# Who orders the side engines' queues: a two-layer hybrid decoder trunk with the order planned by a timeline model

## The chip, the cores and the metric

The kernel runs on one core of a Trainium2 chip. A time is the device time of one execution in microseconds (us). The kernel before took 2891.07 us (median of two runs, 2890.86 and 2891.28). The core has one tensor engine (TensorE, "PE" in the profile), a vector engine (VectorE, "DVE"), an activation engine (ScalarE, "ACT"), GpSimd ("POOL"), and a queue engine that issues DMAs (SyncE, "SP"). Each engine runs its own list of instructions strictly in order; where it needs a result of another engine, the instruction at its head waits on a semaphore, and all behind it wait too.

## The reference, cut to what matters

```python
D_MODEL = 1024; SEQ = 1024; DEPTH = 2; CHUNK = 64     # 4 mLSTM heads and 4 retention heads of 256
def reference(x, c, positions, w_ada, b_ada, norm_g, w_in, conv_w, conv_b, ...):
    c_act = silu(c)
    for l in range(DEPTH):
        shift, scale, gate = split(c_act @ w_ada[l] + b_ada[l], 3)
        h = rmsnorm(x, norm_g[l]) * (1 + scale) + shift
        mq, mk, mv, mo, mz, mi, mf, rq, rk, rv, rz = split_cols(h @ w_in[l])
        mq, mk = split(silu(causal_dwconv(concat(mq, mk), conv_w[l], conv_b[l])), 2)
        cell = mlstm_chunkwise(mq, mk, mv, mi + b_igate[l], mf + b_fgate[l])
        y_m = sigmoid(mo) * head_layernorm(cell, gn_m[l]) * silu(mz)
        ret = retention_chunkwise(rotary(rq, positions), rotary(rk, positions), rv)
        y_r = head_layernorm(ret, gn_r[l]) * silu(rz)
        x = x + gate * (concat(y_m, y_r) @ w_out[l])
    return rmsnorm(x, final_g)
```

Everything is float32. In each chunk the two attentions compute scores q k^T, weight them, multiply by v, add the part that comes from a running state, and update that state with k^T v.

## The kernel before, in words

**Arithmetic.** A float32 product is made of three matmuls in a reduced format (fp32r): each operand is cut into a high half, a cast made by ACT (L742, `split_to`), and a low half, the operand minus its cast, made by POOL unless told otherwise (L743). Then L150, L151 and L152 (`mm3`) multiply high by high, low by high and high by low. So every operand of PE passes over ACT and then over POOL or DVE. Tiles called wH and wL are the halves of weights, cH and cL those of the attention's state, sH and sL those of its weighted scores; the tiles q and kc hold both halves of q and k.

**Projections.** The large product h @ W_in is done two column groups at a time, by a scheme with seven products in place of eight (as in Strassen's method). It needs sums and differences of the blocks of h, the forms F of a layer, built once by DVE (`build_forms`, L566 to L583, tiles b and acc), and sums of the blocks of the weights (`weight_forms`, L597 to L603), by POOL for q and k and by DVE for v and the gates. A `Feeder` keeps four of a group's weight forms ahead. Weights come by the loads L611 (`pair_forms`, tile raw) and L623 (`vpair_forms`, tile b). After each product ACT copies and DVE adds into the accumulators (L646 and L649, `combine`, traced with high priority).

**Jobs.** In each layer PE runs the first gate columns (`first`), the small products for mi and mf (`gate_units`; their weights wgr are loaded in the startup and split there, L424 and L742/L743), and then a list of jobs: v for four pairs of heads; then for heads 4 to 7 (retention) and 0 to 3 (mLSTM) the q and k projections, with one gate job between two heads. A finished q or k passes the rotary (L826 to L832) or the convolution with SiLU (L749 to L759), and is written to DRAM (L797, buffers qdr and kfr; k also in a second form, kdr). When k of a head is done, its attention is launched: a generator whose parts are woven between the PE units of the jobs that follow, by counting ticks.

**A score step.** Each head has four chunks of 256 positions. For chunk j, `fetch_qk` (L857) loads q and k back from DRAM into tiles called acc, ACT casts them (L742), and POOL takes the low halves (L743). q has two buffers, kc has one. `diagonal` (L896) and `mm3` then make the scores on PE. `fetch_kv` loads and splits v and the rows of k. DVE weights the scores (L909 to L920), PE makes the values and the state update, DVE normalises (L1007 to L1029) and `finish` multiplies in the gates and stores (L1034, L1038).

**Ahead of the jobs.** In layer 0 a startup region, an order written out by hand as a script of steps, runs the adaLN product, the first norm and the first gate columns. Then come `build_forms`, the gate chain (`gate_chain`, L454 to L529: the stabiliser of the mLSTM, with a store and a reload through DRAM at L491 and L505), in layer 0 the rotary tables (L391 to L419, from a load of the positions at L391), and the loads of the rotary tables (L840). The end of a layer is the product with W_out (`out_units`), in layer 1 also with the final norm and stores.

**What sets the order.** PE's order is written by hand for the whole kernel, and all engines' order in the startup and in the last part of layer 1:

```python
    manual = ctx.enter_context(tc.manual_schedule(engines={mybir.EngineType.PE}))   # L1256
    startup = tc.manual_schedule()                                                  # L1258
        ending = tc.manual_schedule() if l and alone else None                      # L1123, in out_units
```

Elsewhere the framework's scheduler decides in what order DVE, ACT, POOL and SP get the instructions that the program traces. It lists them by the times at which it reckons that each can start, from the dependences, the buffers that pools hand out and the priorities (which follow the order of tracing, except under `tc.high_priority()` in `combine`). The list is fixed before the run.

## Time and profile before

| | before |
|---|---|
| median of the runs | 2891.07 us |
| the profiled execution, its own time | 2891.24 us |
| its span in the profile | 2889.5 us |
| mean granted PE clock | 0.893 |
| busy PE / DVE / POOL / ACT | 2302.5 / 1826.2 / 1367.5 / 1163.1 us |
| instructions in the span | 35104 |
| DMA | 360.20 MB, mean 125 GB/s |

The profile shows one execution. "Busy" is the sum of an engine's instruction times; a PE that is held at a lower clock is busy for longer with the same work. A row of a view by instruction has the start and the duration in us, the engine, the line of the program, the operation, the output and input tiles and their shapes, and in square brackets how long the engine stood idle before it and what ended that wait ("<-ACT kc L742": the cast of kc at L742 on ACT). By stages: the startup lasts until about 142 us; layer 0 has v until 380, the retention heads until 800, the mLSTM heads until 1310 and the output product until 1445 us; the norm and the first gate columns of layer 1 last until 1582, its v until 1800, the retention heads until 2230, the mLSTM heads until 2680, and the last product, the final norm and the stores until the end.

### The profile page before, as it was taken

How to read it: one execution, taken by the hardware profiler on the slowest of the kernel's cores; microseconds unless marked ns; L12 is line 12 of the kernel's file. 1: busy time of each engine (PE TensorE's matmuls, PEld its weight loads, DVE VectorE, ACT ScalarE, POOL GpSimd, SP SyncE). 2: the span in 40 equal slices, each digit the busy share in tenths (PEclk: the TensorE clock that was granted, in tenths of full speed). 3: DMA queues.
4: the chain of work that ended last, by engine and by line, in shares of the span. 5: the costliest groups of instructions: out<-in, count | busy, mean ns of one | idle time of the engine just before them, and what ended most of it. 6: DMA issues, size and time to landing. Idle time of an engine off the chain costs nothing. (4 is left out here: it accounts for less than half of the span.)

```text
span 2889.5 us, 35104 instructions
## 1 busy us (share of the span) xinstructions
PE 2302.5 (80%) x11483; PEld 1943.4 (67%) x11483; DVE 1826.2 (63%) x3199; ACT 1163.1 (40%) x2149; POOL 1367.5 (47%) x1098
## 2 busy tenths in 40 slices
PE   4789977777676777789996999788777676767998
PEld 3589966556565556668785998666666555656777
DVE  4994356557566777877527534567567677777744
ACT  4523333333344444454345333333334444444433
POOL 0444664544545545452266446655554545544123
PEclk9899989789788888889998999899888788888999
DMA  7034344433443334347641433444343433424766
GB/s 221 25 85 123 95 118 130 117 120 107 122 123 110 114 105 129 94 132 256 220 142 33 107 99 113 121 120 118 98 127 91 111 109 110 129 82 128 234 195 173
DMA packets 483012, 360.20 MB, mean 125 GB/s; under 512 B 186866, under 2 KB 403706, under 8 KB 482828
## 3 DMA queue, kind: packets, MB, share of 16 engines
q1 hardware_dynamic: 482684, 357.70, 42.5%
q8 instruction: 90, 1.47, 0.2%
q14 instruction: 94, 0.77, 0.1%
q10 hardware_dynamic: 144, 0.26, 0.0%
HBM read 251.90 MB, written 105.94 MB: 124 GB/s over the span
## 5 line engine op out<-in xcount | busy, mean ns | idle before, releaser
L743 POOL TENSOR_TENSOR wL<-raw,wH 128x512 fp32r<-128x512 f32 x492 | 674.4, 1378 | 710.8 <-ACT wH L742 655.9
L150 PE MATMUL pp<-b,wH 128*128 128x512 f32 x1616 | 673.7, 417 | 41.6 <-ACT acc L646 36.7
L151 PE MATMUL pp<-b,wH 128*128 128x512 f32 x1616 | 664.1, 411 | 4.2 <-DVE b L1095 4.2
L152 PE MATMUL pp<-b,wL 128*128 128x512 f32 x1616 | 659.8, 408 | 0.0
L742 ACT CAST wH<-raw 128x512 fp32r<-128x512 f32 x556 | 340.4, 618 | 633.3 <-PE pp L151 269.8
L150 PEld LDWEIGHTS pp<-b,wH 128*128 128x128 f32 x1616 | 331.1, 205 | 116.3 <-ACT acc L646 43.9
L151 PEld LDWEIGHTS pp<-b,wH 128*128 128x128 f32 x1616 | 328.6, 203 | 68.9 <-DVE b L1095 5.8
L152 PEld LDWEIGHTS pp<-b,wL 128*128 128x128 f32 x1616 | 324.1, 201 | 73.8
L896 PE MATMUL pa<-q,kc 128*128 128x256 f32 x384 | 105.5, 423 | 169.5 <-POOL q L743 126.2
L150 PE MATMUL pp<-wH,b 128*128 128x256 f32 (+1 forms) x576 | 182.7, 317 | 57.4 <-ACT wH L742 44.4
L649 DVE TENSOR_TENSOR acc<-pp,acc 128x512 f32<-128x512 f32 x180 | 122.4, 681 | 149.6 <-PE pp L152 137.3
L896 PEld LDWEIGHTS pa<-q,kc 128*128 128x128 f32 x384 | 85.0, 306 | 191.3 <-POOL q L743 139.6
L151 PE MATMUL pp<-wL,b 128*128 128x256 f32 (+1 forms) x576 | 182.0, 316 | 13.2 <-POOL wL L743 13.2
L152 PE MATMUL pp<-wH,b 128*128 128x256 f32 (+1 forms) x576 | 181.4, 315 | 0.2
L150 PE MATMUL pa<-wH,b 128*128 128x256 f32 (+1 forms) x576 | 177.1, 307 | 0.0
L151 PE MATMUL pa<-wL,b 128*128 128x256 f32 (+1 forms) x576 | 176.8, 307 | 0.0
L152 PE MATMUL pa<-wH,b 128*128 128x256 f32 (+1 forms) x576 | 176.6, 307 | 0.0
L150 PEld LDWEIGHTS pp<-wH,b 128*128 128x128 f32 x576 | 113.9, 198 | 65.6 <-ACT wH L742 45.4
L754 DVE SCALAR_TENSOR_TENSOR acc<-acc,cols,acc 128x511 f32<-128x511 f32 x144 | 140.3, 974 | 27.2 <-ACT acc L749 26.1
L743 POOL TENSOR_TENSOR wL<-b,wH 128x512 fp32r<-128x512 f32 x56 | 77.3, 1381 | 159.3 <-ACT wH L742 120.4
L646 ACT COPY acc<-pp 128x512 f32<-128x512 f32 x180 | 104.2, 579 | 111.8 <-PE pp L152 106.7
L151 PEld LDWEIGHTS pp<-wL,b 128*128 128x128 f32 x576 | 114.0, 198 | 20.4 <-POOL wL L743 15.2
(348 smaller groups left out, 4954.2 us busy)
## 6 DMA issues: line engine op xcount, KB each, us to landing
raw<-in_w_in_dram SPq DMA_DIRECT2D x250, 256.0 KB
raw<-in_w_out_dram SPq DMA_DIRECT2D x128, 256.0 KB
gdr<-acc SPq DMA_DIRECT2D x64, 256.0 KB
vdr<-acc SPq DMA_DIRECT2D x64, 256.0 KB
qdr<-acc SPq DMA_DIRECT2D x64, 256.0 KB
kfr<-acc SPq DMA_DIRECT2D x64, 256.0 KB
acc<-qdr SPq DMA_DIRECT2D x64, 256.0 KB
acc<-kfr SPq DMA_DIRECT2D x64, 256.0 KB
```

The source lines that it names most:

```text
L150: PE.matmul(o, lt[0], rt[0], start=start, stop=False, skip_group_check=more)
L151: PE.matmul(o, lt[0], rt[1], start=False, stop=False, skip_group_check=more)
L152: PE.matmul(o, lt[1], rt[0], start=False, stop=stop, skip_group_check=more)
L646: A.copy(keep[n], bank["Z" if n == 3 else "X"])
L649: V.tensor_tensor(keep[m], bank[b], keep[m], ALU.add)
L742: A.copy(dst[0], src)
L743: eng.tensor_tensor(dst[1], src, f(dst[0]), ALU.subtract)
L754: V.scalar_tensor_tensor(acc[:, d:], pt[:, 0:HALF - d], wcol, acc[:, d:], ALU.mult, ALU.add)
L896: PE.matmul(pd, piece(kx[j], i, dt, tt * P, P), qd, start=dt == 0 and i == 0, stop=dt == 1 and i == 1)
```

## The change

```diff
-    with tile.TileContext(nc) as tc:
+    with tile.TileContext(nc, schedule_with_timeline_sim=True) as tc:
         tile_hybrid_trunk(tc, *args)
```

This is the whole diff (L1518). It changes what the scheduler reckons with. By default it uses a simple estimate of each instruction's length and readiness; now it plans with a model of the engines' timelines. The program that is traced is the same: the same instructions with the same operands and shapes, the same pools and buffer counts. PE's hand-written order, the startup's script and the last part of layer 1 stay as they are. What may differ is the order of the instructions on DVE, ACT, POOL and SP in all other regions, with it the order in which DMAs are issued, and which of a pool's buffers a tile gets.

## The prediction

> **What bounds the kernel now.** I read the page first, for the whole: the profiled execution took 2891.24 us, 1.7 us outside its span, and the median of the runs shown is 2891.07 us, so a sum made on this execution holds for the median.
>
> ```profile
> span 2889.5 us, 35104 instructions
> PE 2302.5 (80%) x11483; PEld 1943.4 (67%) x11483; DVE 1826.2 (63%) x3199; ACT 1163.1 (40%) x2149; POOL 1367.5 (47%) x1098
> ```
>
> No engine is full. TensorE (PE) is the busiest and its order is the one thing that does not change, so I ask next what it waits for. This is the view of waits for PE alone (total us, times, longest):
>
> ```profile
> PE pa L896 <- POOL q L743: 126.2, 32, 7.7
> PE pa L150 <- ACT kc L742: 123.1, 22, 10.3
> PE pa L976 <- ACT cH L742: 59.0, 13, 8.0
> PE pp L150 <- ACT wH L742: 44.4, 5, 22.8
> PE pa L896 <- POOL kc L743: 43.3, 32, 3.0
> PE pp L150 <- ACT acc L646: 38.7, 17, 8.8
> PE pa L152 <- POOL kc L743: 33.3, 26, 3.0
> PE pa L151 <- POOL q L743: 17.6, 18, 3.1
> ```
>
> Five of these rows are one cause: the first matmuls of a score step wait for the two halves of q and kc, which ACT casts (L742) and POOL subtracts (L743). Together 126.2 + 123.1 + 43.3 + 33.3 + 17.6 = 343.5 us in 64 score steps (8 heads, 4 chunks, 2 layers), 5.4 us each. The windows show where (us of PE, its weight loads, DVE, ACT and POOL busy, then the granted PE clock):
>
> ```profile
> 141.60:235.00 93.40, 74.09 (x551) 71.95 (x552) 81.31 (x140) 24.15 (x44) 39.48 (x26) 0.88 0.34 93
> 380.00:800.00 420.00, 309.56 (x1377) 255.82 (x1377) 246.08 (x414) 139.26 (x265) 218.96 (x173) 0.84 0.41 118
> 800.00:1310.00 510.00, 378.94 (x1721) 313.53 (x1720) 375.14 (x754) 230.12 (x450) 246.70 (x213) 0.86 0.41 118
> 1582.00:1615.00 33.00, 27.46 (x202) 26.36 (x203) 28.35 (x31) 11.61 (x22) 15.10 (x11) 0.91 0.34 78
> 1800.00:2230.00 430.00, 338.39 (x1552) 281.36 (x1551) 271.83 (x471) 163.16 (x308) 239.21 (x194) 0.88 0.40 113
> 2230.00:2680.00 450.00, 325.22 (x1439) 266.23 (x1438) 327.48 (x634) 200.39 (x397) 225.35 (x194) 0.84 0.40 114
> ```
>
> 380 to 800 and 1800 to 2230 are the retention heads, 800 to 1310 and 2230 to 2680 the mLSTM heads. There PE idles a quarter of the time and its clock is at 0.84 to 0.88, while DVE, the next busiest, stands at 59 to 74%.
>
> **Why a score step waits: queues, not work.** The stretch around one stall, PE, ACT and POOL, each in order of time:
>
> ```profile
> 497.24 0.39 PE L152 MATMUL pp<-b,wL 128*128 128x512 f32 x1
> 505.16 0.58 PE L150 MATMUL pa<-q,kc 128*128 128x256 f32 x1 [7.54 <-ACT kc L742]
> ...
> 497.66 0.60 ACT L534 ACTIVATE th<-pp 128x512 f32<-128x512 f32 x1 [1.30 <-PE pp L152]
> 498.15 1.13 ACT L742 CAST wH<-raw 128x512 fp32r<-128x512 f32 x2
> 504.49 0.61 ACT L742 CAST kc<-acc 128x512 fp32r<-128x512 f32 x1
> ...
> 498.89 2.48 POOL L743 TENSOR_TENSOR wL<-raw,wH 128x512 fp32r<-128x512 f32 x2 [11.33 <-ACT wH L742]
> 501.34 1.25 POOL L597 TENSOR_TENSOR raw<-raw,raw 128x512 f32<-128x512 f32 x1
> 502.68 1.26 POOL L598 TENSOR_TENSOR raw<-raw,raw 128x512 f32<-128x512 f32 x1
> ```
>
> POOL stood idle for 11.33 us and then ran four weight operations that are needed only later; the cast of kc waited for them, since a weight cast that needs L598 stands before it on ACT. POOL was idle because ACT's queue held an evacuation (L534) that had to wait for PE's last matmul before the score step, with two casts of weights, long ready, behind it. PE waited for ACT, ACT had waited for PE.
>
> **The change, part by part.** The work and PE's order stay; DVE, ACT, POOL and SP are put in another order. I counted in the two built programs. ACT around this stall (minus before, plus after):
>
> ```
> +L742 TensorCopy wH_4625<-raw_4617 128x512
> ...
> -L534 Activation th_4736<-pp_4511 128x512
> -L742 TensorCopy wH_4625<-raw_4617 128x512
> ...
>  L742 TensorCopy wH_4698<-raw_4617 128x512
> +L534 Activation th_4671<-acc_4642 128x512
>  L742 TensorCopy kc_4651<-acc_4649 128x512
> ```
>
> *Score steps.* For each step I followed the semaphores of the built program back from its first q or kc wait, through every queue, to the latest matmul that must have run, and counted the matmuls between that one and the waiting one. Before, 36 of the 64 steps have 0 or 1 between, so the whole off-PE chain is exposed; the median is 0. After, 8 have, and the median is 24; 45 steps gain, one loses. A stall then shrinks by the time of the added matmuls. Their step is in these rows, after a stall and once warm:
>
> ```profile
> 545.16 0.58 PE L896 MATMUL pa<-q,kc 128*128 128x256 f32 x1 [6.35 <-POOL q L743]
> ...
> 548.04 0.63 PE L150 MATMUL pp<-b,wH 128*128 128x512 f32 x1
> 548.47 0.63 PE L151 MATMUL pp<-b,wH 128*128 128x512 f32 x1
> ...
> 550.95 0.39 PE L152 MATMUL pp<-b,wL 128*128 128x512 f32 x1
> 551.17 0.39 PE L150 MATMUL pp<-b,wH 128*128 128x512 f32 x1
> ```
>
> 0.43 us start to start when cold, 0.22 when warm. I take the warm one, which gives least: 24 x 0.227 = 5.4 us against stalls of 5.4 us on average. Taken off stall by stall, never below zero, it leaves about 140 of the 343.5 us; the same count leaves 49 of the 59 us on cH and about 10 less on L646. Sum: 225 us.
>
> *The clock.* After the 6.35 us stall PE ran cold until 550.5, some 5 us at half pace, so 2.4 us more were lost. 28 steps fewer with an open chain (36 less 8), 2.4 us each: 67 us.
>
> [...]
>
> So 292 us lie open. Not all will come: if PE runs earlier, DVE must give the same work in less time. With all of it the four stretches shrink from 1810 to 1518 us and DVE's 1220 us become 80%, in mLSTM stretches over 85%. DVE can run so full (95% in the row below), but it then answers later. The bounds are 0 and 292; I take 0.7, nearer to the upper end, since DVE has room: -204 us.
>
> *Both fronts.* Here the change costs. Ahead of the first value projection of a layer, DVE builds the forms of h (L566 to L583), and the new order puts the gate chain (L468 to L490) and, in layer 0, rotary tables (L393 to L416) among them; on SP the weight loads of L623 (tile b) now stand behind the gate chain's stores and its reload (L491, L505). By the built programs 62 more DVE instructions precede the last form in layer 0, and 21 in layer 1. Their price, from two windows of DVE alone in which these kinds run:
>
> ```profile
> 138.90:192.40 53.50, 50.95 (x70) 0.88 0.30 75
> 1578.10:1608.50 30.40, 29.99 (x30) 0.84 0.27 80
> ...
> 1578.53 1.96 SPq L623 DMA_DIRECT2D b<-in_w_in_dram  x4
> ...
> 1581.56 0.62 ACT L742 CAST wH<-b 128x512 fp32r<-128x512 f32 x1 [5.61 <-DMA b<-in_w_in_dram]
> ```
>
> 0.73 us each: 62 x 0.73 = 45 us. 1.0 us each: 21 us. One more DMA on the way, 3.0 us from issue to use, each time: +3. But DVE is then done with work that today stalls PE just after: the windows from 141.6 and from 1582 hold 93.4 - 74.1 = 19.3 and 33.0 - 27.5 = 5.5 us of PE idle. Layer 0: 45 + 3 - 19 = +29. Layer 1: 21 + 3 - 5 = +19. Bounds: +72 if nothing is recovered, 0 if hidden behind PE's gate matmuls.
>
> *Startup.* The small gate weights (wgr) arrive late, and their cast and split stand early in the queues:
>
> ```profile
> 46.77 0.31 DVE L743 TENSOR_TENSOR cL<-wgr,cH 128x32 fp32r<-128x32 f32 x2 [29.61 <-ACT cH L742]
> ...
> 60.92 0.48 DVE L331 TENSOR_SCALAR b<-b,rs 128x512 f32<-128x512 f32 x1
> ...
> 48.71 0.50 SPq L391 DMA_DIRECT2D kc<-in_positions_dram  x1
> ```
>
> DVE waits 29.61 us with ready work behind. After, these stand some 30 places later, but the copy of the positions (L393) now comes right after this L331, and its load is issued only at 48.71, usable 3.0 us later, at 51.7. DVE passes that point at 61.4 today: -10 us (bounds 0 and -29.6).
>
> Sum: -204 + 29 + 19 - 10 = -166; 2891 - 166 = 2725 us.
>
> **The rivals.**
> *DVE takes the place of the queues* (0.17). The score steps get their operands, but DVE at 74% in the mLSTM stretches cannot follow, and waits on cf, sd or evacuations replace those on q. Half of my share: -102 + 38 = 2827 us. For it: DVE's rows in the windows. Against: 95% when it has ready work.
> *More comes* (0.15): all 292 us, 2891 - 292 + 38 = 2637 us. For it: I counted the added matmuls at the warm step, and later stalls shrink with earlier ones.
> *Slower* (0.12): the casts of q and kc stand so early on ACT and POOL that the reloads have not landed, and the queues stand for them, with wH, cH and sH behind. It decides from the point where a load lands after its cast's turn by more than the 5.4 us of added cover. Then the 343.5 us stay, the fronts add 38, and at half of 64 steps' 3.0 us landing another 96 come: 2929 to 3025, middle 2975 us. Against: the loads stand hardly later on SP than before.
> *Nothing reaches PE* (0.06): the order differs, but other waits end at the same time: 2891 us. Against: 945 of 3197 DVE instructions move by more than 5 places.
>
> A rule speaks for the DVE rival. The Trainium skill ("SBUF — State Buffer", Who interferes with whom) has a DVE instruction with two SBUF inputs and a GpSimd one that reads SBUF shut each other out for the whole instruction, so tighter packing would lengthen DVE. The trace bears it out:
>
> ```profile
> L566 DVE TENSOR_TENSOR acc<-b,b x32: 671/684/1780, 103.8 to 1570.0; 128x512 f32<-128x512 f32 x32
> ```
>
> The longest is 1.1 us over the median of 0.68 us, about the length of the POOL operations above (1.25 and 1.26 us).
>
> **How the numbers follow.** My forecast has 0.50, with its own range of 2650 to 2800 us. Faster or slower by about 2%, 58 us, is what a measurement of this kernel can tell: under 2833 is faster. Faster: 0.50 + 0.15 + 0.10 of the DVE rival = 0.75. Same: 0.07 + 0.06 = 0.13. Slower: 0.12. The range reaches from under the case of all cover, 2610, to 2870, past the DVE rival; the slower case and part of the last stay out.
>
> **What would show it.** Right: in PE's waits the rows on q and kc fall from 343 to under 180 us, the clock in the four stretches rises over 0.88, and DVE there is over 75% busy. The first L150 matmul on wH after the layer's start comes about 38 us later than 141.6, and the stall before the second layer's grows from 22.8 to over 40 us. DVE's wait of 29.61 us near 47 goes. Wrong: ACT or POOL waiting tens of us for acc<-qdr or acc<-kfr in the heads, or rows on q and kc still over 300 us.

## The result, and the profile after

The changed kernel takes 2694.49 us (median of two runs, 2691.59 and 2697.38), against 2891.07 us before: a ratio of 0.932, with a 95% interval of 0.9277 to 0.9363. The profiled execution took 2697.38 us. The first lines of its page, the span and the busy time of each engine:

```profile
span 2695.7 us, 35179 instructions
PE 2248.0 (83%) x11483; PEld 1902.1 (71%) x11483; DVE 1901.6 (71%) x3199; ACT 1161.9 (43%) x2149; POOL 1385.5 (51%) x1098
```

The matmuls are the same 11483, and PE is busy 54.5 us less: they ran at a higher clock (mean granted clock 0.918, 0.893 before). DVE runs the same 3199 instructions and is busy 75.4 us more. The view of waits for PE (total us, times, longest):

```profile
PE pp L150 <- ACT wH L742: 88.9, 3, 45.4
PE pa L976 <- ACT cH L742: 64.2, 24, 6.8
PE pa L896 <- POOL kc L743: 50.3, 32, 3.7
PE pa L896 <- POOL q L743: 39.8, 18, 5.1
PE pa L152 <- POOL kc L743: 32.6, 21, 3.4
PE pa L150 <- ACT kc L742: 27.2, 9, 5.3
PE pp L150 <- ACT acc L646: 20.0, 13, 6.1
PE pp L150 <- DVE acc L649: 18.1, 10, 3.1
PE pa L976 <- DVE cL L743: 15.2, 8, 3.6
...
PE pa L151 <- POOL q L743: 7.6, 7, 1.6
...
PE pa L896 <- ACT kc L742: 2.6, 1, 2.6
```

The rows on q and kc sum to 160.1 us (343.5 before). The rows on cH and cL did not fall, and the row on wH doubled: its two long waits are the fronts. The four head stretches, cut at the same matmuls as before's windows (length, then us busy of PE, its weight loads, DVE, ACT and POOL, granted clock, DMA share, GB/s):

```profile
387.10:730.50 343.40, 288.39 (x1377) 240.12 (x1378) 267.81 (x419) 139.58 (x267) 222.66 (x174) 0.92 0.51 145
730.50:1193.00 462.50, 370.30 (x1721) 305.73 (x1720) 389.76 (x741) 226.37 (x442) 247.43 (x210) 0.90 0.46 129
1701.00:2089.40 388.40, 326.67 (x1551) 272.36 (x1551) 295.65 (x471) 160.57 (x305) 237.60 (x190) 0.92 0.44 124
2089.40:2493.90 404.50, 318.21 (x1440) 260.62 (x1439) 335.61 (x630) 200.06 (x396) 228.58 (x194) 0.89 0.45 124
```

Together 1598.8 us against 1810.0: 211 us of the gain are here. PE idles 295.2 us (457.9 before, 163 less) and is busy 1303.6 us (1352.1 before, 48.5 less, the clock). DVE is busy 1288.8 us, 81% of the stretches, against 1220.5, with about the same number of instructions (2261 for 2273).

The fronts and the startup. The first value product of each layer, and DVE in the startup, each row with its wait in brackets:

```profile
163.89 0.58 PE L150 MATMUL pp<-wH,b 128*128 128x256 f32 x1 [45.36 <-ACT wH L742]
...
1484.35 0.58 PE L150 MATMUL pp<-wH,b 128*128 128x256 f32 x1 [40.92 <-ACT wH L742]
...
53.57 0.29 DVE L393 CAST q<-kc 128x256 f32<-128x256 int32 x1 [21.51 <-DMA kc<-in_positions_dram]
```

Layer 0's first product starts 22 us later than before (141.6), layer 1's wait is 18 us longer (22.8), and DVE's wait of 29.61 us for the small gate weights has become one of 21.51 us for the positions.

### The profile page after: what moved, and what is told of

Read it like the earlier page. It is cut to its first block, busy times and chain, and to the rows that moved or that the text cites. A ratio compares the mean times of both kernels' runs of the same rounds, so it can differ in the third digit from the quotient of the medians.

```text
span 2695.7 us, 35179 instructions
## 1 busy us (share of the span) xinstructions
PE 2248.0 (83%) x11483; PEld 1902.1 (71%) x11483; DVE 1901.6 (71%) x3199; ACT 1161.9 (43%) x2149; POOL 1385.5 (51%) x1098
## 5 line engine op out<-in xcount | busy, mean ns | idle before, releaser
L743 POOL TENSOR_TENSOR wL<-raw,wH 128x512 fp32r<-128x512 f32 x492 | 692.5, 1414 | 483.4 <-ACT wH L742 461.1
L150 PE MATMUL pp<-b,wH 128*128 128x512 f32 x1616 | 665.7, 412 | 40.8 <-ACT acc L646 20.0
L151 PE MATMUL pp<-b,wH 128*128 128x512 f32 x1616 | 657.7, 407 | 6.6 <-DVE b L1095 6.6
L150 PEld LDWEIGHTS pp<-b,wH 128*128 128x128 f32 x1616 | 324.8, 201 | 115.0 <-ACT acc L646 25.6
L151 PEld LDWEIGHTS pp<-b,wH 128*128 128x128 f32 x1616 | 323.0, 200 | 69.4 <-DVE b L1095 7.3
L150 PE MATMUL pp<-wH,b 128*128 128x256 f32 (+1 forms) x576 | 179.4, 311 | 89.2 <-ACT wH L742 88.9
L649 DVE TENSOR_TENSOR acc<-pp,acc 128x512 f32<-128x512 f32 x180 | 122.0, 679 | 152.0 <-PE pp L152 138.5
L150 PEld LDWEIGHTS pp<-wH,b 128*128 128x128 f32 x576 | 112.2, 195 | 95.2 <-ACT wH L742 89.5
L152 PE MATMUL pp<-wH,b 128*128 128x256 f32 (+1 forms) x576 | 178.8, 310 | 0.0
L896 PE MATMUL pa<-q,kc 128*128 128x256 f32 x384 | 83.1, 350 | 93.5 <-POOL kc L743 50.3
L896 PEld LDWEIGHTS pa<-q,kc 128*128 128x128 f32 x384 | 66.4, 239 | 111.4 <-POOL kc L743 58.2
L646 ACT COPY acc<-pp 128x512 f32<-128x512 f32 x180 | 104.5, 581 | 51.6 <-PE pp L152 51.2
L976 PE MATMUL pa<-cH,q 128*128 128x256 f32 (+1 forms) x384 | 68.1, 302 | 64.3 <-ACT cH L742 64.2
```

The lines of the kernel that those rows point to most:

```text
L150: PE.matmul(o, lt[0], rt[0], start=start, stop=False, skip_group_check=more)
L151: PE.matmul(o, lt[0], rt[1], start=False, stop=False, skip_group_check=more)
L152: PE.matmul(o, lt[1], rt[0], start=False, stop=stop, skip_group_check=more)
L646: A.copy(keep[n], bank["Z" if n == 3 else "X"])
L649: V.tensor_tensor(keep[m], bank[b], keep[m], ALU.add)
L743: eng.tensor_tensor(dst[1], src, f(dst[0]), ALU.subtract)
```

## The experiments

**Which engine's order?** A list of the changed kernel's order was put into the kernel before as edges that fix only the order of issue on one engine and add no wait. The other engines are planned around it by the default estimate, so their order can differ from before's too. The edit, the same for all of these runs but for the engines listed (`perm` is the packed list, `_REGIONS` are the regions ordered by hand, which stay as they are; "..." marks lines left out):

```diff
+_ORDERS = {mybir.EngineType.Activation: (
...
+def pin_orders(tc, nc):
...
+    traced = list(nc.cur_bb.bb.instructions)
+    for engine, text in _ORDERS.items():
...
+        mine = [i for i in traced if i.engine == engine and str(i.opcode) not in _SKIP]
...
+        for a, b in zip(perm, perm[1:]):
+            if any(mine[a].name in r and mine[b].name in r for r in _REGIONS):
+                continue
+            tc.add_manual_dep(mine[b], mine[a].name,
+                              mybir.DependencyInfo(mybir.DependencyClass.NoSync, mybir.DependencyReason.DATA),
+                              reason="order")
...
         tile_hybrid_trunk(tc, *args)
+        pin_orders(tc, nc)
```

*ACT alone.* Its order by itself gives the score steps the same cover as the changed kernel by the count of the prediction.

> The kernel before, with the order of ACT's instructions pinned to that of the changed kernel; DVE, POOL and SP keep the default plan around it. Theory (the casts of q and kc were late in ACT's queue): by the built program 8 of the 64 score steps have 0 or 1 matmul of cover, the median is 24, as in the changed kernel. PE's rows on q and kc fall from 343 to about 160 to 200 us, the head stretches give about what they gave in the changed kernel (-217 us); 10 more DVE instructions stand ahead of the last form of layer 0, 9 of layer 1, so the fronts cost some +10 us: 2650 to 2720 us, about 2685. Rival (the gain needs DVE's or SP's order too): less than half of the gain, 2790 to 2880 us.

*DVE alone.*

> The kernel before, with DVE's order alone pinned to that of the changed kernel. Theory: 31 of 64 score steps stay exposed (36 before), so at some 8 us each 5 steps give -40 us at most; the fronts have the changed kernel's DVE order (62 and 23 more instructions ahead of the last form) and cost +28 and +17 us, part of it won back: 2860 to 2920 us, about 2890. Rival (DVE's order carries the gain): under 2790 us.

*POOL and SP.*

> The kernel before, with POOL's and SP's order pinned to that of the changed kernel. Theory: 43 of 64 score steps are exposed (36 before), since ACT and DVE keep an order that doesn't fit: 7 more stalls at 5 to 8 us each make it slower, 2890 to 2960 us, about 2930. Rival (reloads issued earlier on SP, or POOL's low halves taken earlier, carry the gain): under 2830 us.

Measured: ACT 2949.89 us, ratio 1.0209 (1.0175 to 1.0243); DVE 2965.76 us, 1.0254 (1.0227 to 1.028); POOL and SP 2911.87 us, 1.0069 (1.0046 to 1.0093). ACT's and DVE's order alone make the kernel some 2% slower, POOL's and SP's 0.7%. The last lies in its expected range (2890 to 2960 us); DVE's run is 46 us above the top of its range, and ACT's lies outside both the theory's and the rival's. What these times mix is seen by stretch. The four head stretches with ACT's order alone, cut at the same matmuls:

```profile
405.43:790.32 384.89, 298.71 (x1377) 247.80 (x1375) 256.57 (x413) 134.57 (x263) 214.40 (x172) 0.88 0.43 124
790.32:1314.07 523.75, 385.58 (x1720) 318.57 (x1719) 387.19 (x747) 225.63 (x444) 245.91 (x210) 0.84 0.40 114
1835.41:2274.27 438.86, 346.08 (x1552) 286.86 (x1551) 274.64 (x470) 156.78 (x302) 235.88 (x191) 0.87 0.38 108
2274.27:2719.92 445.65, 329.25 (x1439) 268.23 (x1437) 338.08 (x629) 196.21 (x392) 222.94 (x194) 0.85 0.40 113
```

Together they are 1793.2 us against 1810.0: 17 us of gain in the heads, where the changed kernel has 211. PE's rows on q and kc did fall, from 343.5 to 227.6 us, but those on cH and cL rose from 65.0 to 144.2. Outside the heads 76 us are lost: the first value product starts at 181.5 us, 40 us later than before (some 10 were expected for both fronts; the reason stays open), and what lies behind the last head takes 20 us more. ACT itself shows what holds the heads back. Its waits for reloads from DRAM, over the whole run; first with its order alone, then in the changed kernel, then before:

```profile
ACT v L733 <- DMA acc<-vdr: 175.7, 33, 12.5
ACT q L742 <- DMA acc<-qdr: 136.0, 38, 10.4
ACT b L786 <- DMA acc<-kdr: 49.9, 12, 6.5
ACT kc L742 <- DMA acc<-kfr: 33.5, 23, 6.6
ACT b L791 <- DMA acc<-kdr: 29.4, 13, 5.9
```

```profile
ACT q L742 <- DMA acc<-qdr: 84.7, 30, 6.8
ACT v L733 <- DMA acc<-vdr: 68.9, 35, 5.7
ACT kc L742 <- DMA acc<-kfr: 17.9, 19, 2.3
ACT b L791 <- DMA acc<-kdr: 6.5, 6, 1.9
ACT b L786 <- DMA acc<-kdr: 1.1, 3, 0.5
```

```profile
ACT q L742 <- DMA acc<-qdr: 23.1, 14, 4.1
ACT v L733 <- DMA acc<-vdr: 6.6, 6, 3.7
ACT kc L742 <- DMA acc<-kfr: 3.4, 3, 2.1
```

Sums: 424.5, 179.1 and 33.1 us. The changed order takes reloaded operands early; with ACT's order alone the reloads do not come early, and the queue stands. One such place, SP, DVE and then ACT, with ACT's order alone:

```profile
662.80 1.47 SPq L1038 DMA_DIRECT2D ndr<-zt  x3
674.15 0.95 SPq L797 DMA_DIRECT2D qdr<-acc  x2
675.14 0.46 SPq L866 DMA_DIRECT2D acc<-vdr  x1
675.65 1.98 SPq L778 DMA_DIRECT2D acc<-kdr  x4
...
672.36 1.76 DVE L830 TENSOR_TENSOR acc<-acc,th 128x512 f32<-128x512 f32 x1
...
678.32 0.91 ACT L733 ACTIVATE v<-acc,kc 128x256 fp32r<-128x256 f32 x2 [11.87 <-DMA acc<-vdr]
```

The reload of v (L866) needs nothing from the stores of q (L797), but SP issues it at 675.14, behind two of them that wait for the rotary's last steps on DVE (L830). ACT stands 11.87 us. The same reload in the changed kernel:

```profile
614.84 1.84 SPq L1038 DMA_DIRECT2D ndr<-zt  x4
617.05 0.38 SPq L866 DMA_DIRECT2D acc<-vdr  x1
619.27 1.79 SPq L778 DMA_DIRECT2D acc<-kdr  x4
624.32 1.55 SPq L797 DMA_DIRECT2D qdr<-acc  x2
...
619.87 0.91 ACT L733 ACTIVATE v<-acc,kc 128x256 fp32r<-128x256 f32 x2 [3.55 <-DMA acc<-vdr]
```

Here SP issues it ahead of those stores, and ACT waits 3.55 us. So I asked which second order makes ACT's pay.

> The kernel before, with ACT's and SP's order pinned to that of the changed kernel; DVE keeps an order planned around them (545 of its 3197 instructions stand over 5 places from the changed kernel's). With ACT's order alone, ACT stood 207 us in layer 0's heads for reloads (vdr 82.9, qdr 75.3, kdr 48.7). Theory C (the early casts lack early reloads, which SP's order gives): ACT's waits for reloads fall under 120 us there, the heads gain over 100 us, total 2700 to 2800 us. Theory B (reloads and states hang on DVE, whose results SP's stores and ACT's casts wait for): DVE's order is still the wrong one, ACT goes on waiting, total 2850 to 2960 us.

> The kernel before, with ACT's and DVE's order pinned to that of the changed kernel; POOL follows within 0.3 places, SP has 113 of 1826 DMAs over 5 places off. Theory B (ACT's early casts need DVE's results in the same order): nearly all of the gain is there, 2690 to 2760 us, and PE's rows on cL and on acc fall to the changed kernel's size. Theory C (SP's order gives it): 2850 us or more, with ACT still waiting over 180 us for reloads in layer 0's heads.

> The kernel before, with the order of ACT, DVE and SP pinned to that of the changed kernel; POOL differs by 0.28 places in the mean. Every theory that holds the order for the cause expects the changed kernel's time: 2680 to 2710 us. Rival (pinning costs something, or buffers are dealt out otherwise): over 2730 us; then the times of the pinned kernels can't be read as those of the orders.

> The kernel before, with DVE's and SP's order pinned to that of the changed kernel; ACT keeps a default plan around them. Measured so far: ACT and SP 2827, ACT and DVE 2896, all three 2716 us. By the built program 31 of 64 score steps stay exposed. Theory D (the three orders only pay together, each missing one costs over 100 us): 2820 to 2960 us. Rival (ACT's order is of no use in itself, since alone it made the kernel slower): 2700 to 2780 us.

> The kernel before, with all four orders pinned to the changed kernel's; control for the 21 us between the three pinned orders (2715.73 us) and the changed kernel (2694.49 us). If POOL's small differences made them: 2685 to 2702 us. If the pins do (buffers dealt out otherwise, added waits): 2708 to 2725 us.

The results, with the head stretches cut at the same matmuls, the sums of PE's rows on q and kc and on cH and cL, and ACT's waits for reloads summed as above:

| order pinned | us | ratio to before (95%) | heads, us | PE on q, kc | PE on cH, cL | ACT on reloads |
|---|---|---|---|---|---|---|
| none (before) | 2891.07 | 1 | 1810.0 | 343.5 | 65.0 | 33.1 |
| ACT | 2949.89 | 1.0209 (1.0175 to 1.0243) | 1793.2 | 227.6 | 144.2 | 424.5 |
| DVE | 2965.76 | 1.0254 (1.0227 to 1.028) | 1829.8 | 271.7 | 128.5 | 68.4 |
| POOL, SP | 2911.87 | 1.0069 (1.0046 to 1.0093) | 1790.0 | 305.5 | 82.0 | 15.3 |
| ACT, DVE | 2896.05 | 1.0006 (0.9995 to 1.0016) | 1762.7 | 207.2 | 100.2 | 405.1 |
| ACT, SP | 2827.15 | 0.9778 (0.976 to 0.9796) | 1686.2 | 156.6 | 125.9 | 185.7 |
| DVE, SP | 2906.51 | 1.0039 (1.0026 to 1.0053) | 1799.7 | 299.0 | 97.2 | 38.2 |
| ACT, DVE, SP | 2715.73 | 0.9391 (0.9366 to 0.9416) | 1613.6 | 161.0 | 71.9 | 170.2 |
| all four | 2700.58 | 0.933 (0.9313 to 0.9346) | 1602.8 | 155.4 | 81.8 | 178.6 |
| none (the changed kernel) | 2694.49 | 0.932 (0.9277 to 0.9363) | 1598.8 | 160.1 | 79.4 | 179.1 |

Pinning itself costs nothing that can be told from zero: all four give the changed kernel's ratio. The three orders without POOL's came out at 2715.73 us, just above the 2680 to 2710 that every theory expected. SP's order more than halves ACT's wait for reloads, with or without DVE's (424.5 to 185.7, 405.1 to 170.2 us); it does not end it. With ACT's and SP's order PE's rows on q and kc stand where the changed kernel has them, and the heads gain 124 of the 211 us. DVE's order then gives the heads 73 us more, and the rows on the state fall; first with ACT and SP, then with DVE added:

```profile
PE pa L976 <- ACT cH L742: 72.3, 19, 11.1
PE pa L976 <- DVE cL L743: 53.6, 22, 9.3
```

```profile
PE pa L976 <- ACT cH L742: 54.9, 25, 5.9
PE pa L976 <- DVE cL L743: 17.0, 12, 3.7
```

Taking one order away from the three, and leaving that engine to the default plan, costs 180 us (SP), 191 us (ACT) or 111 us (DVE); in the heads alone 149, 186 and 73 us. Theory C was right on SP: without its order the time stays over 2850 us (2896.05), with it over 100 us came in the heads. But 2827.15 us is above its 2800, since this run loses some 57 us outside the heads and lacks DVE's order. Theory B missed both of its times; it was right only that DVE's order is worth over 100 us more once the other two are there. Theory D's price, over 100 us for each missing order, held; that the three pay only together did not, since ACT and SP alone gain 2.2%. POOL's order, 0.28 places off in the mean, is worth the last 15 us; through which instructions stays open.

**Raising the score operands alone.** The mechanism of the prediction, in the kernel before; the new line stands over the five lines of the loop's body:

```diff
             for dst, dr, tag, bufs in ((qs, qdr, "q", 2), (kx, kfr, "kc", 1)):
...
+                with tc.high_priority():
...
```

> The kernel before under the default plan, with only the reloads of q and k, their casts and low halves (the body of the loop of fetch_qk) traced at high priority. By the built program 19 score steps have 0 or 1 matmul of cover (36 before, 8 in the changed kernel). Counting alone (the prediction's way): 17 steps at 5.4 + 2.4 us make -130 us, 2740 to 2800 us. Theory B (operands come early only where DVE's order goes with it): the reloads wait on SP behind stores that wait for DVE, or the casts hold up others on ACT; -30 to +60 us, 2860 to 2950 us.

Measured 2872.20 us, ratio 0.9933 (0.9917 to 0.995): a gain of about 20 us, 36 in the heads, where the count promised 130. It lies in the range of theory B. PE's rows on q and kc fell only from 343.5 to 289.7 us, and those on cH and cL rose from 65.0 to 86.6. The count takes the waits on other queues, between the last matmul that a chain needs and its end, for nothing; which of them came in here stays open.

**The fronts.** In the changed kernel, DVE's instructions of the gate chain and of the rotary tables are kept behind the last form (in the order of the file: the rotary tables, the gate chain twice, the helper, the last form):

```diff
+            behind_forms(V.tensor_copy(ang, pos.bitcast(I32)))
...
+            behind_forms(V.scalar_tensor_tensor(lf[0:4], lf[0:4], 0.0, e[0:4], ALU.min, ALU.subtract))
...
+            behind_forms(V.tensor_scalar(liq[0:4], li[32:36], MAG_Q, -MAG_Q, ALU.add, ALU.add))
...
+    def behind_forms(ins):
+        tc.add_manual_dep(ins.ins, last_form[0].ins.name,
+                          mybir.DependencyInfo(mybir.DependencyClass.NoSync, mybir.DependencyReason.DATA))
...
+            last_form[0] = V.tensor_tensor(t4, t4, b22, ALU.subtract)
```

> The changed kernel, with the DVE instructions of the gate chain and of the rotary tables kept behind the last of the layer's forms (an order edge only, no work changed); 145 DVE instructions then stand ahead of the end of layer 0's last form and not 230, in layer 1 25 fewer. Theory (the gate chain and the tables ahead of the forms cost the fronts): the wait of 45.4 us for the first value weights falls to some 10 to 20 us, the one before layer 1's first value product to some 20 us, DVE's wait of 21.5 us for the positions goes: 2694 - 28 - 18 = 2648, less some 5 to 15 us that DVE's later work takes back: 2640 to 2670 us. Rival (DVE is what bounds the stretches after a front, so the work only moves): 2685 to 2700 us.

Measured 2668.10 us, ratio 0.9224 (0.92 to 0.9248), 26 us under the changed kernel. The first value products of the two layers:

```profile
135.17 0.58 PE L150 MATMUL pp<-wH,b 128*128 128x256 f32 x1 [21.93 <-ACT wH L748]
...
1448.57 0.58 PE L150 MATMUL pp<-wH,b 128*128 128x256 f32 x1 [18.27 <-ACT wH L748]
```

The time lies in the expected range. The waits fell from 45.36 and 40.92 us to 21.93 and 18.27, together 46 us, and DVE's wait for the positions is gone. Of this, 20 us were given back (5 to 15 expected), as the two v stretches take 19 and 11 us longer and the heads 10 less. Adding the raised priority of the score operands to it:

> The changed kernel with the fronts mended as in the run before (gate chain and rotary tables behind the forms, 2668.1 us) and the reloads, casts and low halves of q and k traced at high priority under the timeline plan. By the built program the score steps' mean cover goes from 22.7 to 23.1 matmuls, with the same 8 exposed steps, so next to nothing is left to win there: 2655 to 2675 us. Rival (the raised priority puts casts ahead of their reloads, as under ACT's order alone): 2690 us or more.

Measured 2665.13 us, 0.9214 (0.9198 to 0.9231): not to be told from the kernel with the mended fronts, as expected. Under the timeline plan, raising these reloads further gains nothing that can be measured.

**How near DVE is to the bound.**

```diff
-            V.transpose(z.rearrange(...), nrm[j].rearrange(...))
+            for _ in range(3):
+                V.transpose(z.rearrange(...), nrm[j].rearrange(...))
```

> The changed kernel with the fronts mended (2668.1 us), and in finish the transpose of a chunk's result (L1034 of the changed kernel, 64 times 0.705 us, needed by stores only) done three times in place of once: 128 more DVE instructions, 90 us of DVE work in the heads, the same result; the score steps' mean cover goes from 22.7 to 20.6 matmuls. It asks how near DVE is to setting the time, at 81% busy in the changed kernel's heads. If DVE has taken the bound: 2668 + 90 = 2758 us, or more. If its 310 us of idle time there still take such work: under 2690 us. Between, the slope is the price of a us of DVE work.

Measured 2709.52 us, 0.9372 (0.9348 to 0.9397), 41 us more than with the mended fronts alone. The transposes with the addition, as a group of the view by lines:

```profile
L1041 DVE STREAM_TRANSPOSE zt<-n 128x512 f32<-128x512 f32 x192 | 134.6, 701 | 18.3 <-ACT n L1035 13.1 <-DMA kdr<-th 3.4
```

In the kernel with mended fronts alone this group has 64 instructions and 45.1 us. So 134.6 - 45.1 = 89.5 us were added and 41.4 us came through, 0.46 us for each us of DVE work that only stores need (about 0.4 to 0.6 by the two intervals). DVE does not set the time, but it is no longer free. The planned order changed with the addition too (mean cover 20.6 for 22.7), so part of the 41 us may be that.

## Why the prediction was right, and where its reasons were not

**The time.** 2725 us were forecast, 2694.49 came; the range of 2610 to 2870 holds it.

**Heads: right in size, in part by luck.** -204 us were forecast and 211 came, 0.72 of the 292 us where 0.7 was taken. The 0.7 was chosen between two bounds and not worked out, so that it was met this closely is luck, the more so as the rows that gave the time are not quite those that were counted (below). The split holds as well: idle time fell 163 us against 0.7 x 225 = 158, busy time by the clock 48.5 us against 0.7 x 67 = 47. The clock's term had about the right price and number. Taking for a cold spell a run of matmuls that start over 1.5 times as far apart as warm ones of their shape, and lose over 0.8 us by it, the head stretches hold 73 before and 54 after, and one costs 2.0 us in the mean: 19 fewer, some 38 of the 48.5 us, against 0.7 x 28 = 20 at 2.4 us. The Trainium skill ("TensorE: Matmul & The Clock Gate", HAM oscillation) has, for a kernel of another shape, 1.67 us of throttled time at each stall, half of which is lost. By that the term would be 0.7 x 28 x 0.84 = 16 us, an estimate; this trace decides for the larger price.

**Which stalls fell: partly wrong.** The rows on q and kc fell by 183 us, more than the 142 that 0.7 of the counted 203 would be. For cH the count took about 10 us off and left 49 of 59.0 (its 225 is 203 + 10 + 10, rounded up); the row became 64.2, and cL rose from 6.0 to 15.2. The rows on L646 gave 19 us (10 counted), and those on L649 took 11. The states are made by PE's update, DVE and ACT in a chain. In the runs their rows rise to 125.9 us with ACT's and SP's order, and DVE's order brings them back to 71.9, near the 65.0 of before.

**The signs.** Those named for right came: 160.1 us on q and kc (under 180), the clock at 0.89 to 0.92 (over 0.88), DVE at 76 to 84% in the four stretches (over 75%), the stall ahead of layer 1's v at 40.92 us (over 40). The first value product came 22 us later, not 38. But a sign named for wrong came as well: ACT waits 84.7 us for acc<-qdr in the changed kernel, 23.1 before. It was no sign of a slow kernel: PE's rows on q and kc fell all the same.

**The step that failed: cover by count as a cause.** The prediction followed semaphores back to the last matmul and read the exposed steps off that. ACT's order alone has the same count, 8 exposed of 64 and a median of 24. It took 116 us off the rows on q and kc, where the changed kernel took 183, put 79 us on those on cH and cL, and left the heads 17 us shorter. The count says how early PE lets a chain begin, not when the queues in it move. What it left out is what the rival "slower" named: casts that stand ahead of their reloads. That rival had 0.12, on the ground that the loads stand hardly later on SP than before. To stand no later was not enough: with ACT's order alone ACT waited 424.5 us for reloads. What spared the changed kernel most of it (179.1 us) is that SP's order moved with ACT's, and what brought the waits for the states down again is DVE's order. The number was right with half of its reason.

**Fronts: right mechanism, mis-sized in layer 0.** Forecast +29 and +19. In layer 1 the wait grew 18 us (24 forecast), and 1 us was won back in the v stretch (5 forecast): +17. In layer 0 the first product starts 22 us later, about 28 against the end of the startup, where 48 were forecast; 16 came back by the end of v (19 forecast). The term that was mis-sized is 62 x 0.73 us. It priced the added DVE instructions as if all were in the way; some of them, from the row at 53.57 on, ran in the startup already, between the script's steps. In the two traces 28 more DVE instructions start ahead of the startup's last matmul, and 44 more between it and the first value product: 44 x 0.73 = 32 us, near the 28 that were measured. The run with mended fronts shows that these instructions are the cause of most of the added wait in both layers.

**Startup: right sign.** -10 forecast. The last matmul of the startup starts at 118.3 us against 124.3: -6. As forecast, the next wait was the one for the positions. The rest of the gain, some 6 us, had no term: the last product and the stores took 8 us less, the output product of layer 0 took 2 more.

**DVE rival: half present.** DVE's busy time in the heads rose by 68 us with about the same instructions, to 81% of the time, and added DVE work shows at 0.46. How much of the 81 us that did not come is DVE's stays open; the 0.3 that was set aside covers all of it.

## What to carry to other kernels

An order is worth what it is worth together with the other queues' orders. Moving a consumer's cast ahead on one engine pays in full only if the load that feeds it is ahead on its own queue, and that load can stand behind a store that waits for a third engine. Read such a run by stretch: ACT's order alone is 2% slower as a whole, and yet its heads are a little shorter. Before moving one thing up, list the waits for DMA of the engine that will run it; and when a planner's new order wins, look at the short stretches that it made worse (here the front of each layer), since a few order edges gave 26 us more at no cost.

## What the runs showed of the hardware that I had not expected

DVE instructions of one form got longer as the engines were packed more tightly. Two groups by line, before and after, with shortest, median and longest in ns:

```profile
L793 DVE SCALAR_TENSOR_TENSOR b<-acc,b x48: 382/420/1518, 403.8 to 2183.1; 128x256 fp32r<-128x256 f32 x48
```

```profile
L793 DVE SCALAR_TENSOR_TENSOR b<-acc,b x48: 403/885/1601, 398.6 to 2039.2; 128x256 fp32r<-128x256 f32 x48
```

The groups of L649 (first row before, second after), one of whose inputs is in PSUM, kept their mean of 0.68 us:

```profile
L649 DVE TENSOR_TENSOR acc<-pp,acc 128x512 f32<-128x512 f32 x180 | 122.4, 681 | 149.6 <-PE pp L152 137.3 <-ACT acc L646 10.0 <-issue 1.3
...
L649 DVE TENSOR_TENSOR acc<-pp,acc 128x512 f32<-128x512 f32 x180 | 122.0, 679 | 152.0 <-PE pp L152 138.5 <-ACT acc L646 10.0 <-DMA acc<-qdr 3.4
```

L793 reads two operands from SBUF; its median went from 420 to 885 ns. This is the side that the Trainium skill's rule speaks of ("SBUF — State Buffer", Who interferes with whom): a DVE instruction with two SBUF inputs and a GpSimd one that reads SBUF shut each other out. The traces agree with it instruction by instruction. Of L793's 96 instructions in the two, 54 overlap one of GpSimd and last up to 1.60 us; 42 overlap none, and the longest of these takes 0.43 us. L649 takes 0.69 us at most, with an overlap or without. The L830 above, at 1.76 us where 0.68 is usual without an overlap, is of the same kind. No run took the GpSimd work away.
